# Norm gains moved behind the transposes, the identity built on GpSimd, and one product moved to other PSUM banks in a two-layer hybrid decoder

## Chip, cores and metric

The kernel runs on one core of a Trainium2 chip. The metric is device microseconds (us) of one execution. The core's engines are named as the profile names them: PE (TensorE), with PEld for its weight loads, DVE (VectorE), ACT (ScalarE), POOL (GpSimd) and SP (SyncE, here the queue that issues nearly all DMAs). Each engine takes its own instructions strictly in order.

## What is computed

Two layers of a decoder on x (256 x 1024, fp32), with a fixed memory mem (256 x 1024). Cut to what matters here:

```python
for l in range(2):
    h = rmsnorm(x, norm_g[l])
    z = h @ w_in[l]                       # 1024 -> 7968, split into many parts
    mem_kv = rmsnorm(mem, mem_norm_g[l]) @ w_mem_kv[l]   # 1024 -> 1024: keys, values
    o_a = nsa(z parts); o_b = fox(z parts); o_m = cross_attention(z part, mem_kv)
    u = sum of gate_i * (o_i @ w_branch_i[l])
    x = x + u @ w_out[l]

def rmsnorm(x, g): return x * rsqrt(mean(x * x) + 1e-6) * g
```

`norm_g` and `mem_norm_g` are the gains: one number for each of the 1024 columns and each layer.

## The kernel before

All products are fp32 in three passes. Each operand is split into a high part (fp32r) and the rest, and PE adds high x high, low x high and high x low (`gemm_steps`, lines 224, 225, 226). ACT makes the high part of a weight (line 160) and DVE the low part (line 161), two weight chunks ahead of their use. A weight chunk is 256 rows x 512 columns, 512 KB, in one of four `wraw` buffers that SP fills (line 140). A product of 1024 rows (`gemm`) is four such steps, each of 12 PE instructions, for two row tiles t of 128 tokens. Its sums lie in banks of the pool `pmm`, of which there are three. `pS` is another pool, of two banks, for scores; `pT` has two for transposes.

The activation has to stand transposed, columns on partitions. `to_T` does four PE transposes (line 329) of one row tile into one bank. Then ACT writes the high part (line 315) and DVE the low part (line 317), 512 elements wide.

The gain is a factor per column, so before the transpose it is a factor along the free axis. `gain_rows` therefore loads it broadcast to all 128 partitions, 256 KB per half. DVE multiplies mem by it in `mem_norm` (line 359) and x by it and by the row's rstd in `norm_x` (line 566). The row factor rstd of mem is applied to the results of the product. `mem_norm` also takes the sums of squares on ACT (line 372).

The order of the program: mem is loaded, normalised and transposed; `mem_kv` makes the memory's keys K and then its values V, both 1024 x 512. Beside them `norm_x` squares x on ACT (line 560), POOL makes rstd (lines 295, 296), DVE scales x and PE transposes it to hT. Then the parts of `ORDER` follow: K2 (416 columns), K1 (384), Q, and so on. After K of the memory, `on_k` squares the four heads on ACT (line 307), POOL makes their factor (lines 295, 296, 298), and DVE multiplies the bank out (line 394), which frees it. V needs two banks while K holds two of the three. So the first row tile of V can run at once and the second waits for line 394. POOL also builds the rope tables Ct and St (lines 548 to 550) in that time.

In K2 and K1, `rope_k` multiplies with the tables on DVE (lines 336 to 338) and adds the two parts on POOL (line 339). One tick later DVE multiplies by rstd (line 589), and PE transposes (line 593). The code is a list of Python calls with `later` for delayed pieces; a scheduler then sets the final order of each engine's instructions from dependencies and its own estimates.

Of the kernel before, what the change touches and what calls it, by code (L numbers as in the profile page):

```python
# [58 lines left out]
def hybrid_kernel(ctx: ExitStack, tc, I, cst_d, out_d):  # L59
# [181 lines left out]
    def gain_rows(ap, offset):  # L241

        h = [S([128, 512], tag, bufs=2) for tag in ("PTh", "PTl")]
        for i in range(2):
            nc.sync.dma_start(h[i], bcast(ap, 128, offset + i * 512, 512))
        return h

    gb0 = [S([128, 512], tag, bufs=2) for tag in ("PTh", "PTl")]
    for i, c in enumerate((0, 512)):
        nc.sync.dma_start(mrow0[:, 0, c:c + 512], I["mem"][0, 0:128, c:c + 512])  # L250
        nc.sync.dma_start(gb0[i], bcast(I["mem_norm_g"], 128, c, 512))
        if c == 0:
            nc.scalar.dma_start(cst[:, 0:128], cst_d[:, 0:128])
    nc.sync.dma_start(mrow0[:, 1], I["mem"][0, 128:256, :])
    load_w()
    load_w()
# [88 lines left out]
    def mem_load():  # L345
        mrow = S([128, NT, D], "big")
        gb = gain_rows(I["mem_norm_g"], D)
        nc.sync.dma_start(mrow, I["mem"][0].rearrange("(t p) d -> p t d", p=128))
        return mrow, gb

    def mem_norm(mrow, gb, spread):

        mT = act_pair(8, "aT")
        rm = []
        for t in range(NT):
            xn = S([128, D], "t4", bufs=2)
            for k0 in (0, 4):
                ks = slice(k0 * 128, k0 * 128 + 512)
                nc.vector.tensor_tensor(xn[:, ks], mrow[:, t, ks], gb[k0 // 4], op=ALU.mult)

                def f(xn=xn, t=t, k0=k0):
                    to_T(mT, xn[:, k0 * 128:k0 * 128 + 512], t, k0)
                if spread:
                    later(1 + 2 * t + k0 // 4, f)
                else:
                    f()
        def stats():
            for t in range(NT):
                ss = S([128, 1], "ssx", bufs=4)
                for j in range(2):  # L370
                    s2 = S([128, 1], "ssx2", bufs=4)
                    nc.scalar.activation(SQ()[:, :512], mrow[:, t, j * 512:(j + 1) * 512], AF.Square, accum_out=s2)
                    if j == 0:
                        s1 = s2
                nc.gpsimd.tensor_tensor(ss, s1, s2, op=ALU.add)
                rm.append(rstd_of(ss, D, "rm"))
            mark("mem")
        if spread:
            later(5, stats)
        else:  # L380
            stats()
        return mT, rm
# [788 lines left out]
```

## Time and profile before

| what | us |
|---|---|
| median of 3 runs (lowest, highest) | 654.85 (653.78, 655.8) |
| the profiled execution | 653.95 |
| its span in the trace | 652.2 |
| PE busy (share of the span) | 630.8 (97%) |
| DVE / ACT / POOL busy | 485.8 / 388.4 / 187.7 |

The span is from the first to the last instruction of the trace; the time of the same execution is 1.75 us longer. PE is the engine to watch: where it has no gap, no other engine's work is seen in the time. A product counts as busy until its modelled end, so the time from one start to the next is the better price of one product in a dense stretch.

### The profile page before, as it was taken

To read this page: it belongs to the slowest core of one execution; us is meant where nothing else is said; L and a number is where in the kernel's file an instruction comes from. 1 tells how busy PE (TensorE), PEld (TensorE's weight loads), DVE (VectorE), ACT (ScalarE), POOL (GpSimd) and SP (SyncE) were. 2 spreads that over 40 slices of the span, in tenths; PEclk is the share of its full clock that TensorE was granted. 3 is DMA by queue.
4 is the path that set the end of the run, shared out by engine and by line. 5 is a ranking of instruction groups with operands and counts; after the bars stand their busy time and mean duration, and the time that the engine had idled before them with its cause. 6 is when DMAs were issued, how large, how long until landed. Compare 5 with 4: busy or idle time off the path is not lost.

```text
span 652.2 us, 10316 instructions
## 1 busy us (share of the span) xinstructions
PE 630.8 (97%) x3590; PEld 539.8 (83%) x3590; DVE 485.8 (74%) x834; ACT 388.4 (60%) x817; POOL 187.7 (29%) x254
## 2 busy tenths in 40 slices
PE   5899999999998999999999999999999899999997
PEld 3688998878997888888888889987889788888886
DVE  5667889857887976856776689895598777777563
ACT  5656568654666766644566665865457475655441
POOL 2804522343222330703022234330043041133030
PEclk9999999999999999999999999999999999999999
DMA  8856556865442555465646475476644245545542
GB/s 301 216 159 182 190 162 193 201 191 171 130 120 60 154 154 161 135 222 191 215 144 182 148 224 159 135 221 172 189 141 118 65 135 158 161 130 162 162 144 83
DMA packets 74324, 106.64 MB, mean 164 GB/s; under 512 B 16032, under 2 KB 28704, under 8 KB 74272
## 3 DMA queue, kind: packets, MB, share of 16 engines
q1 hardware_dynamic: 74128, 105.92, 54.7%
q8 instruction: 28, 0.46, 0.3%
q14 instruction: 24, 0.20, 0.1%
q10 hardware_dynamic: 144, 0.07, 0.0%
HBM read 104.92 MB, written 1.05 MB: 162 GB/s over the span
## 4 chain that ended last, share of the span: by engine, by line
PE 94%; DVE 2%; POOL 2%; ACT 1%; DMA 1%; issue 0%; SPq 0%; DVEq 0%; POOLq 0%
PE mm L224 21%; PE mm L225 21%; PE mm L226 21%; PE mm L743 4%; PE O L423 4%; PE mm L746 4%; PE mm L745 3%; PE T L472 3%; PE T L329 1%; PE S L224 1%; PE S L225 1%; PE S L226 1%; PE S L916 1%; PE S L1084 1%; DMA PTl<-in_mem_norm_g_dram 1%; PE S L918 1%
## 5 line engine op out<-in xcount | busy, mean ns | idle before, releaser
L161 DVE TENSOR_TENSOR wlo<-wraw,whi 128x1024 fp32r<-128x1024 f32 (+2 forms) x184 | 232.2, 1267 | 94.2 <-ACT whi L160 89.9
L160 ACT ACTIVATE whi<-wraw 128x1024 fp32r<-128x1024 f32 (+2 forms) x184 | 191.2, 1044 | 129.5 <-PE mm L225 81.2
L224 PE MATMUL mm<-whi,aTh 128*128 128x512 f32 (+2 forms) x512 | 203.9, 398 | 5.8 <-DVE sg L728 2.9
L225 PE MATMUL mm<-whi,aTl 128*128 128x512 f32 (+2 forms) x512 | 200.5, 392 | 0.0
L226 PE MATMUL mm<-wlo,aTh 128*128 128x512 f32 (+2 forms) x512 | 194.6, 394 | 0.5 <-DVE wlo L161 0.5
L466 POOL TENSOR_TENSOR P<-P,d 128x512 f32<-128x512 f32 (+1 forms) x64 | 63.8, 1014 | 185.7 <-DVE d L458 83.1
L224 PEld LDWEIGHTS mm<-whi,aTh 128*128 128x128 f32 x512 | 97.3, 190 | 23.9 <-DVE sg L728 3.7
L226 PEld LDWEIGHTS mm<-wlo,aTh 128*128 128x128 f32 x512 | 96.8, 189 | 19.1 <-DVE wlo L161 1.3
L225 PEld LDWEIGHTS mm<-whi,aTl 128*128 128x128 f32 x512 | 97.1, 190 | 17.3
L743 PE MATMUL mm<-aTh,whi 128*128 128x256 f32 x192 | 54.5, 286 | 0.0
L745 PE MATMUL mm<-aTl,whi 128*128 128x256 f32 x192 | 54.3, 285 | 0.0
L455 ACT ACTIVATE P<-S,m 128x256 f32<-128x256 f32 (+1 forms) x112 | 47.0, 431 | 11.4 <-DVE m L452 8.2
L746 PE MATMUL mm<-aTh,wlo 128*128 128x256 f32 x192 | 52.8, 282 | 0.0
L994 POOL TENSOR_TENSOR big<-big,t 128x512 f32<-128x512 f32 x16 | 27.3, 1719 | 74.2 <-DVE t L993 74.1
L315 ACT ACTIVATE PTh<-T 128x512 fp32r<-128x512 f32 (+1 forms) x48 | 27.0, 563 | 23.8 <-PE T L472 23.5
L224 PE MATMUL mm<-whi,oTh 128*128 128x512 f32 x96 | 38.3, 404 | 0.0
L226 PE MATMUL mm<-wlo,oTh 128*128 128x512 f32 x96 | 38.2, 403 | 0.0
L225 PE MATMUL mm<-whi,oTl 128*128 128x512 f32 x96 | 38.0, 396 | 0.0
L743 PEld LDWEIGHTS mm<-aTh,whi 128*128 128x128 f32 x192 | 36.2, 188 | 0.4
L745 PEld LDWEIGHTS mm<-aTl,whi 128*128 128x128 f32 x192 | 36.2, 189 | 0.2
L746 PEld LDWEIGHTS mm<-aTh,wlo 128*128 128x128 f32 x192 | 35.7, 189 | 0.1
L452 DVE TENSOR_REDUCE m<-S 128x2 f32<-128x512 f32 (+3 forms) x64 | 31.8, 512 | 2.6 <-PE S L1084 2.4
(237 smaller groups left out, 986.1 us busy)
## 6 DMA issues: line engine op xcount, KB each, us to landing
wraw<-in_w_in_dram SPq DMA_DIRECT2D x112, 512.0 KB, 3.7
wraw<-in_w_mem_kv_dram SPq DMA_DIRECT2D x16, 512.0 KB, 5.2
wraw<-in_w_out_dram SPq DMA_DIRECT2D x16, 512.0 KB, 3.9
wraw<-in_w_branch_a_dram SPq DMA_DIRECT2D x16, 256.0 KB, 4.2
wraw<-in_w_branch_b_dram SPq DMA_DIRECT2D x8, 512.0 KB, 3.6
wraw<-in_w_branch_m_dram SPq DMA_DIRECT2D x8, 512.0 KB, 3.6
wraw<-in_w_in_dram SPq DMA_DIRECT2D x8, 408.0 KB, 3.7
wraw<-in_w_in_dram SPq DMA_DIRECT2D x8, 384.0 KB, 3.3
```

The source lines that it names most:

```text
L160: nc.scalar.activation(wh[:, :, :n], v[:, :, :n], AF.Copy)
L161: nc.vector.tensor_tensor(wl[:, :, :n], v[:, :, :n], wh[:, :, :n].bitcast(F32), op=ALU.subtract)
L224: nc.tensor.matmul(o_, hi[:, kg, ts], wh[:, k, :n], start=(kg == 0), stop=False)
L225: nc.tensor.matmul(o_, lo[:, kg, ts], wh[:, k, :n], start=False, stop=False)
L226: nc.tensor.matmul(o_, hi[:, kg, ts], wl[:, k, :n], start=False, stop=last and k == 1)
L452: nc.vector.tensor_reduce(m[:, n:n + c], heads(sp[:, o_:o_ + w * c], c), axis=AXX, op=ALU.max, negate=True)
L455: nc.scalar.activation(self.P[:, k], sp[:, k], AF.Exp, bias=m[:, n:n + 1], accum_out=d[:, n:n + 1])
L466: nc.gpsimd.tensor_tensor(P3, P3, b3(d[:, n:n + c], c, w), op=ALU.mult)
L743: nc.tensor.matmul(o_, ch, hi[:, kg, :], start=(kg == 0 and j % 2 == 0), stop=False, skip_group_check=True)
L745: nc.tensor.matmul(o_, ch, lo[:, kg, :], start=False, stop=False, skip_group_check=True)
L746: nc.tensor.matmul(o_, cl, hi[:, kg, :], start=False, stop=(kg == 7), skip_group_check=True)
L994: nc.gpsimd.tensor_tensor(uv, uv, tn, op=ALU.add)
```

## The change

It has five parts.

1. The gains of both norms and layers are loaded as 32 rows of 128 by two small DMAs on ACT's queue and turned once by PE into `gk`, 128 partitions x 32. `to_T_scaled` replaces `to_T` for mem and x: four transposes (two column blocks of both row tiles) go to one bank; then, for each block of 256 elements, ACT and DVE apply the gain as a scale per partition while they write high and low. The multiplications of line 359 and the broadcast loads go; x is scaled by rstd alone.
2. The identity is no longer loaded. POOL fills it with ones and `affine_select` keeps the diagonal.
3. mem comes in four column groups of 256 KB, alternating with the first three weight chunks; the first chunk comes and is split in two halves. Of the four transpose groups the first stands ahead of the memory's K product, and the other three are called within it. Eight products of zeros (`WARM`) stand ahead of everything on PE.
4. The squares of mem are taken once and kept for layer 1. They stand behind the four groups' code.
5. K1's sums lie in the two `pS` banks, and the add of `rope_k` moves from POOL to DVE.

```diff
+WARM = 8
@@ load_w
+        if not loaded:
+            for j in range(2):
+                nc.sync.dma_start(v[:, j], spec[0][j * 128:(j + 1) * 128])
+            spec = []
+            n = 512
@@ split_w
-        nc.scalar.activation(wh[:, :, :n], v[:, :, :n], AF.Copy)
-        nc.vector.tensor_tensor(wl[:, :, :n], v[:, :, :n], wh[:, :, :n].bitcast(F32), op=ALU.subtract)
+        for j in (slice(0, 1), slice(1, 2)) if not parts else (slice(0, k),):
+            nc.scalar.activation(wh[:, j, :n], v[:, j, :n], AF.Copy)
+            nc.vector.tensor_tensor(wl[:, j, :n], v[:, j, :n], wh[:, j, :n].bitcast(F32), op=ALU.subtract)
@@ gemm_steps
+            if t == 0 and within:
+                within.pop(0)()
@@ start of the program (was: mem and gains in halves, the identity by DMA, two weight chunks)
+    grow = S([32, 128], "tm", bufs=2)
+    for i, nm in enumerate(("mem_norm_g", "norm_g")):
+        nc.scalar.dma_start(grow[i * 16:(i + 1) * 16, :], I[nm].rearrange("l (k p) -> (l k) p", p=128))
+    nc.gpsimd.memset(cst[:, 0:128], 1.0)
+    nc.gpsimd.affine_select(out=cst[:, 0:128], in_=cst[:, 0:128], pattern=[[-1, 128]], compare_op=ALU.is_equal,
+                            fill=0.0, base=0, channel_multiplier=1)
+    for g in range(4):
+        mem_cols(mrow0, g)
+        if g < 3:
+            load_w()
+    zero = S([128, 512], "P", bufs=2, dt=F32R)
+    nc.vector.memset(zero.bitcast(F32), 0.0)
+    zp = pS()
+    for _ in range(WARM):
+        nc.tensor.matmul(zp, zero[:, 0:128], zero, start=True, stop=True)
...
+    gk = S([128, 32], "gk")
+    gp = pT()
+    nc.tensor.transpose(gp[:, 0:32], grow, ident[0:32, 0:32])
+    nc.vector.tensor_copy(gk, gp[:, 0:32])
+    def to_T_scaled(dst, src, g, gain):
+        hi, lo = dst[:2]
+        q = pT()
+        for k in range(2):
+            for t in range(NT):
+                nc.tensor.transpose(q[:, (k * 2 + t) * 128:(k * 2 + t + 1) * 128],
+                                    src(t)[:, (g * 2 + k) * 128:(g * 2 + k + 1) * 128], ident)
+        for k in range(2):
+            kg, s = g * 2 + k, q[:, k * 256:(k + 1) * 256]
+            gc = gain[:, kg:kg + 1]
+            nc.scalar.activation(hi[:, kg, :], s, AF.Copy, scale=gc)
+            nc.vector.scalar_tensor_tensor(lo[:, kg, :], s, gc, hi[:, kg, :].bitcast(F32), op0=ALU.mult, op1=ALU.subtract)
@@ rope: its add is (eng or nc.gpsimd); rope_k passes nc.vector
@@ mem_norm (layer 0: group 0 at once, 1 to 3 in `within`; layer 1: later(1 + g))
+        for g in range(4):
+            def f(g=g):
+                to_T_scaled(mT, lambda t: mrow[:, t, :], g, gk[:, l * 8:l * 8 + 8])
+    def mem_stats(mrow):
+        res = []
+        for t in range(NT):
+            ss = S([128, 1], "ssx", bufs=4)
+            nc.scalar.activation(S([128, D], "t4", bufs=2), mrow[:, t, :], AF.Square, accum_out=ss)
+            res.append(rstd_of(ss, D, "rm"))
+        return res
@@ norm_x
+            xn = [S([128, D], "t4", bufs=2) for t in range(NT)]
             for t in range(NT):
-                        nc.vector.scalar_tensor_tensor(xn[:, ks], x[t][:, ks], r, gb[k0 // 4],
-                                                       op0=ALU.mult, op1=ALU.mult)
+                later(1 + t, lambda t=t, r=r: nc.vector.tensor_scalar(xn[t], x[t], r, None, op0=ALU.mult))
+            for g in range(4):
+                later(3 + g, lambda g=g: to_T_scaled(hT, lambda t: xn[t], g, gk[:, 16 + l * 8:24 + l * 8]))
@@ run_k1
-            gemm(hT, 8, on_k1)
+            gemm(hT, 8, on_k1, bank=pS)
```

The scheduler's order moves with it, at three places. On POOL at the program's start (`cst` holds the identity in its first 128 columns, `ISA` is an instruction that the build puts ahead of the first POOL operation other than a memset), before:

```order
L272 MEMSET mhalf_75 128x16
L488 MEMSET kcT_79 128x64
L493 MEMSET KL_81 64x512 x2
L508 MEMSET gcol_153 128x4
L540 MEMSET fg_157 128x1
L780 MEMSET sTv_1579 128x128
L863 MEMSET ce_1651 128x128
L375 ISA
L375 TENSOR_TENSOR ssx_120<-ssx2_121,ssx2_124 128x1
```

and changed:

```order
L263 MEMSET cst_61 128x128
L291 MEMSET mhalf_90 128x16
L518 MEMSET kcT_98 128x64
L523 MEMSET KL_100 64x512 x2
L264 ISA
L264 AFFINE_SELECT cst_61<-cst_61 128x128
```

The `ISA`, which stood ahead of the first sum of squares, now stands ahead of the selection that makes the identity.

On ACT before, from the last transposed groups of mem to K's squares (`T_105`, `T_113` are mem's groups, `whi_205` is weight chunk 4):

```order
L160 ACTIVATE whi_169<-wraw_71 128x1024
L315 ACTIVATE aTh_84<-T_105 128x4x128
L160 ACTIVATE whi_173<-wraw_73 128x1024
L315 ACTIVATE aTh_84<-T_113 128x4x128
L160 ACTIVATE whi_177<-wraw_142 128x1024
L160 ACTIVATE whi_205<-wraw_144 128x1024
L560 ACTIVATE t4_193,ssx_194<-x0_77 128x1024
L560 ACTIVATE t4_199,ssx_200<-x1_78 128x1024
L160 ACTIVATE whi_225<-wraw_223 128x1024
```

and changed (`T_105`, `T_165`, `T_204` are the transposed groups 0, 1, 2 of mem; `big_62` is mem; chunk 4, `whi_194`, comes next):

```order
L168 ACTIVATE whi_145<-wraw_69 128x512 x2
L368 ACTIVATE aTh_103<-T_105,gk_94 128x256
L168 ACTIVATE whi_151<-wraw_73 128x1024
L368 ACTIVATE aTh_103<-T_165,gk_94 128x256
L368 ACTIVATE aTh_103<-T_105,gk_94 128x256
L168 ACTIVATE whi_155<-wraw_76 128x1024
L368 ACTIVATE aTh_103<-T_165,gk_94 128x256
L410 ACTIVATE t4_115,ssx_114<-big_62 128x1024
L410 ACTIVATE t4_121,ssx_120<-big_62 128x1024
L588 ACTIVATE t4_180,ssx_182<-x0_92 128x1024
L368 ACTIVATE aTh_103<-T_204,gk_94 128x256
L588 ACTIVATE t4_181,ssx_187<-x1_93 128x1024
```

The squares of mem, which ACT did first, now stand behind the first two groups of mem, with the squares of x close behind them and half of mem's evacuation still to come. On DVE in the same place, before:

```order
L317 TENSOR_TENSOR aTl_85<-T_105,aTh_84 128x4x128
L161 TENSOR_TENSOR wlo_174<-wraw_73,whi_173 128x1024
L317 TENSOR_TENSOR aTl_85<-T_113,aTh_84 128x4x128
L161 TENSOR_TENSOR wlo_178<-wraw_142,whi_177 128x1024
L161 TENSOR_TENSOR wlo_206<-wraw_144,whi_205 128x1024
L566 SCALAR_TENSOR_TENSOR t4_193<-x0_77,rx_196,PTh_149 128x512
L566 SCALAR_TENSOR_TENSOR t4_193<-x0_77,rx_196,PTl_150 128x512
L566 SCALAR_TENSOR_TENSOR t4_199<-x1_78,rx_202,PTh_149 128x512
L566 SCALAR_TENSOR_TENSOR t4_199<-x1_78,rx_202,PTl_150 128x512
L161 TENSOR_TENSOR wlo_226<-wraw_223,whi_225 128x1024
```

and changed:


```order
L169 TENSOR_TENSOR wlo_156<-wraw_76,whi_155 128x1024
L369 SCALAR_TENSOR_TENSOR aTl_104<-T_165,gk_94,aTh_103 128x256
L369 SCALAR_TENSOR_TENSOR aTl_104<-T_204,gk_94,aTh_103 128x256
L590 TENSOR_SCALAR t4_180<-x0_92,rx_184 128x1024
L590 TENSOR_SCALAR t4_181<-x1_93,rx_189 128x1024
L169 TENSOR_TENSOR wlo_195<-wraw_192,whi_194 128x1024
L369 SCALAR_TENSOR_TENSOR aTl_104<-T_204,gk_94,aTh_103 128x256
```

DVE had chunk 4's low part (`wlo_206`) and all low parts of mem ahead of the scaling of x. Now chunk 4 (`wlo_195`) and the low part of mem's column block 5 (the last row) stand behind both scalings of x.

On PE at the end of K1's first row tile before (`mm_580` and `mm_581` are K1's two row tiles, `T_627` and `T_667` transposes of K2's keys):

```order
L225 MATMUL mm_580<-whi_584,aTl_162 128x384
L226 MATMUL mm_580<-wlo_585,aTh_161 128x384
L593 MATMUL T_627<-cst_61,t2_541 128x128
L593 MATMUL T_667<-cst_61,t2_566 128x128
L224 MATMUL mm_581<-whi_506,aTh_161 128x384
L225 MATMUL mm_581<-whi_506,aTl_162 128x384
L226 MATMUL mm_581<-wlo_507,aTh_161 128x384
L224 MATMUL mm_581<-whi_506,aTh_161 128x384
```

and changed (`S_593` and `S_594` are K1's two row tiles, `T_640` is the first of the same transposes):

```order
L235 MATMUL S_594<-wlo_598,aTh_137 128x384
L233 MATMUL S_594<-whi_597,aTh_137 128x384
L234 MATMUL S_594<-whi_597,aTl_138 128x384
L235 MATMUL S_594<-wlo_598,aTh_137 128x384
L616 MATMUL T_640<-cst_61,t2_554 128x128
L233 MATMUL S_593<-whi_624,aTh_137 128x384
L234 MATMUL S_593<-whi_624,aTl_138 128x384
L233 MATMUL S_594<-whi_624,aTh_137 128x384
```

Both row tiles of K1 now run together. The first of the two transposes stands behind three quarters of K1, the second behind the first two products of Q.

## Rows read from the trace of the kernel before

**Rows 1.** Page, part 1: busy us (share of the span) and instructions of PE.

```profile
PE 630.8 (97%) x3590; PEld 539.8 (83%) x3590; DVE 485.8 (74%) x834; ACT 388.4 (60%) x817; POOL 187.7 (29%) x254
```

**Rows 2.** Windows: stretch, us, busy us (instructions) by engine, PEclk, DMA.

```profile
0.00:12.07 12.07, 4.15 (x16) 2.87 (x17) 4.00 (x7) 6.14 (x13) 3.92 (x18) 1.00 0.79 267
...
14.25:24.05 9.80, 9.80 (x44) 7.88 (x42) 6.95 (x9) 5.22 (x10) 5.17 (x12) 1.00 0.83 233
26.60:31.75 5.15, 2.48 (x12) 1.47 (x11) 3.19 (x5) 4.60 (x13) 4.69 (x13) 1.00 0.94 296
50.00:60.00 10.00, 8.47 (x48) 8.04 (x47) 6.97 (x29) 7.78 (x28) 3.48 (x6) 1.00 0.49 150
190.00:210.00 20.00, 18.02 (x107) 15.26 (x106) 14.73 (x31) 11.44 (x22) 4.50 (x9) 1.00 0.28 68
368.00:380.00 12.00, 10.49 (x56) 9.53 (x55) 10.05 (x36) 8.88 (x32) 4.91 (x8) 1.00 0.51 149
...
640.00:652.20 12.20, 8.39 (x37) 6.46 (x35) 3.90 (x5) 0.88 (x1) 0.00 (x0) 1.00 0.23 86
```

**Rows 3.** Waits of PE: line <- releaser: us in total, times, longest.

```profile
PE T L593 <- DVE t L589: 2.3, 2, 1.2
```

**Rows 4.** Timeline of PE, first products: start us, us, line, op, tiles.

```profile
12.07 0.80 PE L224 MATMUL mm<-whi,aTh 128*128 128x512 f32 x1
```

**Rows 5.** Timeline of PE, 24 to 25 us.

```profile
24.28 1.03 PE L329 MATMUL T<-cst,t 128*128 128x128 f32 x8
```

**Rows 6.** Timeline of PE, the start of K2.

```profile
41.54 0.36 PE L224 MATMUL mm<-whi,aTh 128*128 128x416 f32 x1
```

**Rows 7.** Timeline of ACT, the first memory quarter landed.

```profile
4.04 0.63 ACT L372 ACTIVATE sq<-big 128x512 f32<-128x512 f32 x1 [1.60 <-DMA big<-in_mem_dram]
```

**Rows 8.** Timeline of POOL, the program's start.

```profile
2.23 0.20 POOL L863 MEMSET ce<- 128x128 f32 x1
7.46 0.19 POOL L375 TENSOR_TENSOR ssx<-ssx,ssx 128x1 f32<-128x1 f32 x1 [5.04 <-ACT sq L372]
...
8.01 1.00 POOL L296 TENSOR_TENSOR rm<-rm,mhalf 128x1 f32<-128x1 f32 x1
```

**Rows 9.** Groups by form, ACT, 0 to 60 us: busy us, mean ns.

```profile
L160 ACT ACTIVATE whi<-wraw 128x1024 fp32r<-128x1024 f32 x10 | 10.4, 1054 | 7.7 <-DMA wraw<-in_w_mem_kv_dram 4.3 <-PE mm L225 3.4
L315 ACT ACTIVATE aTh<-T 128x512 fp32r<-128x512 f32 x8 | 4.6, 584 | 0.5 <-PE T L329 0.5
```

**Rows 10.** Groups by form, DVE, 0 to 60 us.

```profile
L161 DVE TENSOR_TENSOR wlo<-wraw,whi 128x1024 fp32r<-128x1024 f32 x9 | 11.0, 1224 | 5.2 <-ACT whi L160 5.2
L317 DVE TENSOR_TENSOR aTl<-T,aTh 128x512 fp32r<-128x512 f32 x8 | 5.4, 683 | 0.0
...
L566 DVE SCALAR_TENSOR_TENSOR t<-x,rx,PTh 128x512 f32<-128x512 f32 x2 | 1.6, 776 | 1.2 <-POOL rx L296 1.2
```

**Rows 11.** DMA issues, 0 to 40 us: count, KB each, median us to landing.

```profile
x<-in_x_dram SPq DMA_DIRECT2D x2, 512.0 KB, 10.3
```

**Rows 12.** Timeline of ACT, end of the squares of x.

```profile
19.27 0.19 ACT L560 ACTIVATION_READ_ACCUMULATOR t<-x 128x1 f32 x1
```

**Rows 13.** Timeline of DVE, the scaling of x behind them.

```profile
21.21 0.80 DVE L566 SCALAR_TENSOR_TENSOR t<-x,rx,PTh 128x512 f32<-128x512 f32 x1 [0.44 <-POOL rx L296]
```

**Rows 14.** Timeline of POOL, key statistics of the memory product.

```profile
28.90 0.19 POOL L295 TENSOR_SCALAR rmk<-ss 128x4 f32<-128x4 f32 x1
...
30.66 0.31 POOL L298 TENSOR_SCALAR rmk<-rmk,rm 128x4 f32<-128x4 f32 x1
```

**Rows 15.** Timeline of PE, value product of row tile 1.

```profile
31.75 0.51 PE L224 MATMUL mm<-whi,aTh 128*128 128x512 f32 x1 [1.48 <-DVE t L394]
```

**Rows 16.** Timeline of PE, the key transpose and K1's second row tile.

```profile
55.24 0.30 PE L593 MATMUL T<-cst,t 128*128 128x128 f32 x1 [1.16 <-DVE t L589]
55.91 0.42 PE L224 MATMUL mm<-whi,aTh 128*128 128x384 f32 x1 [0.36 <-DVE fz L622]
```

**Rows 17.** Windows as in group 2: behind the wait in layer 1.

```profile
519.10:522.60 3.50, 3.47 (x9) 2.71 (x10) 2.23 (x6) 2.34 (x7) 0.00 (x0) 0.53 0.00 0
```

More of the change, by code (lines that the diff above doesn't have):

```diff
@@ L178, in hybrid_kernel @@
     conts, units, pipe = [], [], [None, None]
+    within = []
     done_ = set()
@@ L228, in gemm_steps, with gemm @@
                 consume(t, o_)
+            if t == 0 and within:
+                within.pop(0)()
         tick()
-    def gemm(act, kk, consume, between=None):
-        pp = [pmm(), pmm()]
+    def gemm(act, kk, consume, between=None, bank=None):
+        bank = bank or pmm
+        pp = [bank(), bank()]
         for g in range(kk // 2):
@@ L240, in hybrid_kernel, with mem_cols @@
     mrow0 = S([128, NT, D], "big")
[L241 to L256, printed above, removed]
+    def mem_cols(mrow, g):
+        cs = slice(g * 256, (g + 1) * 256)
+        nc.sync.dma_start(mrow[:, :, cs], I["mem"][0].rearrange("(t p) d -> p t d", p=128)[:, :, cs])
+    grow = S([32, 128], "tm", bufs=2)
[13 more added lines that the diff above has]
+        nc.tensor.matmul(zp, zero[:, 0:128], zero, start=True, stop=True)
     off = [0]
@@ L338, in rope @@
         nc.vector.tensor_tensor(tmp[:, :, 32:64], src[:, :, 0:32], St[:, :, 32:64], op=ALU.mult)
-        nc.gpsimd.tensor_tensor(dst, dst, tmp, op=ALU.add)
+        (eng or nc.gpsimd).tensor_tensor(dst, dst, tmp, op=ALU.add)
     def tb(ap, nh):
@@ L346, in mem_load, with mem_norm @@
         mrow = S([128, NT, D], "big")
[L347 to L351, printed above, removed]
+        for g in range(4):
+            mem_cols(mrow, g)
+        return mrow
+    def mem_norm(l, mrow):
         mT = act_pair(8, "aT")
-        rm = []
-        for t in range(NT):
[L356 to L382, printed above, removed]
+        for g in range(4):
+            def f(g=g):
+                to_T_scaled(mT, lambda t: mrow[:, t, :], g, gk[:, l * 8:l * 8 + 8])
+                if g == (3 if l else 0):
+                    mark("mem")
+            if l:
+                later(1 + g, f)
+            elif g:
+                within.append(f)
+            else:
+                f()
+        return mT
+    def mem_stats(mrow):
+        res = []
+        for t in range(NT):
+            ss = S([128, 1], "ssx", bufs=4)
+            nc.scalar.activation(S([128, D], "t4", bufs=2), mrow[:, t, :], AF.Square, accum_out=ss)
+            res.append(rstd_of(ss, D, "rm"))
+        return res
     def mem_kv(l, mT, rm):
@@ L493, in hybrid_kernel @@
         nc.gpsimd.memset(KL[(1 - g) * 64:(2 - g) * 64, g].bitcast(F32), 0.0)
-    mT, rm = mem_norm(mrow0, gb0, False)
-    load_w()
-    load_w()
+    mT = mem_norm(0, mrow0)
+    rm = mem_stats(mrow0)
     for t in range(NT):
@@ L556, in norm_x @@
         def norm_x():
+            xn = [S([128, D], "t4", bufs=2) for t in range(NT)]
             for t in range(NT):
[L558 removed]
                 ss = S([128, 1], "ssx", bufs=4)
[L560 removed]
+                nc.scalar.activation(xn[t], x[t], AF.Square, accum_out=ss)
                 r = rstd_of(ss, D, "rx")
[L563 to L570 removed]
+                later(1 + t, lambda t=t, r=r: nc.vector.tensor_scalar(xn[t], x[t], r, None, op0=ALU.mult))
+            for g in range(4):
+                later(3 + g, lambda g=g: to_T_scaled(hT, lambda t: xn[t], g, gk[:, 16 + l * 8:24 + l * 8]))
+            later(6, lambda: mark(("h", l)))
         later(1, norm_x)
@@ L585, in rope_k @@
             kr = heads(T2()[:, :128], 2)
-            rope(kr, heads(p, 2), 2, tb(Ct[:, t, i, :], 2), tb(St[:, t, i, :], 2))
+            rope(kr, heads(p, 2), 2, tb(Ct[:, t, i, :], 2), tb(St[:, t, i, :], 2), nc.vector)
             def s1():
@@ L1138, in hybrid_kernel @@
             if l == 0 and (n, g) == (1, 1):
-                mrow, gbm = mem_load()
+                mrow = mem_load()
                 box = []
-                later(1, lambda: box.append(mem_norm(mrow, gbm, True)))
+                later(1, lambda: box.append(mem_norm(1, mrow)))
         if l == 0:
-            mT, rm = box[0]
+            mT = box[0]
     while conts or units or pipe[0] or pipe[1]:
```

11 lines of the change are left out of this document (1 added, 10 removed).

## Prediction, made before the changed kernel ran

> **What bounds the kernel now.** I read the page's busy shares first. PE is busy for 630.8 of 652.2 us [rows 1], so all that can be won without removing products is its 21.4 us of gaps. The windows show where they lie [rows 2]: 7.92 us before the first product at 12.07 (PE works 4.15 of them, on transposes), 2.67 us from 26.60 to 31.75, 1.53 us from 50 to 60 and 1.51 us from 368 to 380, 1.98 us from 190 to 210, and 3.81 us at the end. A gap of the kind of 190 to 210 returns in layer 1 at 510 to 523. The view of PE's waits then gives the causes. The gaps near 55 and 375 are the transpose of line 593, which waits twice for DVE's line 589, 2.3 us in all [rows 3]; behind it K1's second row tile waits for a bank that K2 still holds, 0.36 us [rows 16]. At 31.75 the second row tile of V waits for line 394, which frees its bank [rows 15].
>
> The change touches the first gap, the one at 27 to 32, and the two near 55 and 375. I leave the ends of the layers and the gap at 190 to 210 as they are: the orders of PE and DVE around it are the same in both programs.
>
> **The start, step by step.** What is removed here is the path from the broadcast gains over DVE's multiplications to the transposes. The first quarter of mem had landed when ACT started at 4.04 [rows 7]. The changed kernel's first memory group has the same size and the same place in the queue, so I take 4 us for it, too.
>
> The new condition is the identity. POOL's memsets ahead of the `ISA` end at about 2.3 us: in the row they end at 2.43, and the changed order has one 128x128 memset more and four fewer in front. What the `ISA` takes is in no row. POOL's next operation came 5.04 us after the memsets and was released by ACT, so the `ISA` lies between nothing and 5.04 [rows 8]. I take the long end, as nothing in the row shows it shorter: 7.3. The selection itself lies between a memset of 128x128, 0.20, and the first power, 1.00 [rows 8]; I take 0.4, near the memset, whose size it has. The identity is there at 7.75.
>
> The Trainium skill's page GPSIMD Engine Reference, section Instruction dispatch, says that the first call to freshly loaded POOL code costs about 6 us more and shows no instruction of its own. The trace's 5.04 is below that; by the page's figure all that follows would be 0.9 us later, and the estimate 650.3.
>
> Then the turn of the gains and its copy (0.4, an estimate), four transposes (0.5, half of eight in 1.03 [rows 5]) and one evacuation. A 512-wide one takes 0.58 [rows 9], so I put a 256-wide one at 0.4. The first product starts at 9.1, against 12.07 [rows 4].
>
> That gain of 3 us is not kept, because ACT becomes the queue that counts. In the changed order, from the first evacuation to the square of x's second row tile, ACT has five evacuations (2.0), two weight splits (2.1, 1.05 each [rows 9]) and four squares. A square has the width of a split; with its read of the sum (0.19 [rows 12]) I count 1.14, so 4.6. That makes 8.7 us from 8.65, and the last square ends at 17.3. From the end of the same square (19.27 + 0.19 [rows 12]) to DVE's scaling (21.21 [rows 13]) POOL took 1.75 us, so DVE starts at 19.05. The scaling of 1024 elements lies between one and two passes of line 566 (0.78 each [rows 10]); I take 1.2. Then come chunk 4's low part, 1.22 [rows 10], and a 256-wide low part, which I put at 0.45 from 0.68 for 512 [rows 10]. This is mem's block 5, and it is ready at 21.9.
>
> PE needs that block after 34 products and two groups of transposes. One product takes 0.23 us from start to start (44 products touch 9.80 us [rows 2]), so PE would be there at 9.1 + 7.8 + 1.0 = 17.9. **A new wait of about 4 us** appears inside the first product. It also covers what the clock costs: if the first ten products run at the lower level of 1.2 GHz, where nine took 3.47 us [rows 17], that is some 2 us. The eight products of zeros fit into PE's empty first 6 us and cost nothing.
>
> From 21.9 to the end of K's first row tile PE has 18 products and a group of transposes: 26.6. ACT's four squares of the keys take 1.5 us (four instructions of about 0.37). POOL's factor takes 2.1 us [rows 14], 0.3 of it for work that now stands ahead, so 1.8. Line 394 and the handover take 0.8 (30.97 to 31.75 [rows 14, 15]). The bank is free at 30.7, where it was at 31.75. PE's own path reaches the same place at 30.3, so both agree. Behind it stand 30 products and two transpose groups, 7.9 us, until K2 starts: 38.6. Two groups of transposes that were ahead of K2 before are still to come, 1.0. That makes 39.6, against 41.54 [rows 6]. **The start gives 1.9 us.**
>
> Its ends: were the `ISA` free, ACT could start 2.6 us sooner, and the start would give 4.5. With the selection at 1.00 it gives 1.3.
>
> **K2 to K1.** With K1 in the score banks its second row tile waits for nothing, and the transposes stand 6 us behind K2. The add of 0.45 to 1.15 us on POOL becomes four adds of some 0.29 on DVE per layer, which stand behind chunk 3's low part and ahead of chunk 4's. No unit uses the score banks until Q is done. Both gaps go: 1.53 + 1.51 = **3.0 us** [rows 2]. What hides DVE's extra 1.2 us is PE's work on K1, 48 products; if that cover is gone, it is paid once per layer.
>
> **At nothing.** The multiplications of mem and x in layer 1, the broadcast loads and the second squares of mem lay beside PE's full stretches. The added halves of the evacuations, 16 per layer, lengthen ACT by some 0.2 each there, and ACT is busy 60% [rows 1]. In layer 1 hT needs both row tiles, but 22 us of K and V stand in front of its use.
>
> **Sum.** 1.9 + 3.0 = 4.9 us. The profiled execution took 653.95, 1.75 more than its span; the median is 654.85. I set the sum against the middle of the two, 654.4: 649.5, and 0.1 less for rounding up the gaps: **649.4 us**.
>
> **Rivals.** (A) GpSimd is later than its row allows, for instance because its code comes while all DMA queues are full: half as long again, 7.5 us, is 2.5 later. The start gives nothing or loses 0.6: 652. For it: the row's 5.04 was bounded by ACT and not by POOL; against it: POOL then began at once. The page named above speaks for this side.
>
> (B) The K1 gap moves instead of going. DVE is then the pace-maker between K2 and Q: with four adds and all of K1's rope behind Q's low parts, PE waits for a low part of Q for as long as it waited for the transpose. Only the start is left: 652.5. For it: DVE's own share is 70% in 50 to 60 and 84% in 368 to 380 [rows 2]. Against it: the changed order has the low parts of K1's last chunk and Q's first ahead of K1's rope.
>
> (C) The identity is early (the `ISA` takes next to nothing). The start gives 4.5: 646.8. If besides the low clock behind layer 1's wait stays away, it is 645.2: PE there ran 3.50 us at a granted 0.53, which is about the lower level of 1.2 GHz, after the wait that ended at 519.1, and lost 3.50 x 0.47 = 1.6 us [rows 17]. Layer 0's gap of the same kind kept 1.00 [rows 2]. So a run may have this loss once, twice or not at all. The new wait of 4 us may bring one more, 651.
>
> (D) **Slower.** ACT is in order, and the square of x stands ahead of the evacuation of mem's third group. If x lands late, ACT stands still, and with it PE. A tile of x landed 10.3 us after its issue at about 6 to 7 us [rows 11], so near 17, and 1 MB of mem, 1.5 MB of weights and no broadcast gains now stand ahead of it: some 14 us. Each us past 16.2 is paid in full. It turns slower by over 0.3% (2 us, about what a measurement of this kernel can tell from no change) where x's second tile lands 6.9 us later, after 23; at 25 the time is 658. Against it: less is queued ahead of x than before.
>
> **How the numbers follow.** My forecast 0.58, A 0.14, B 0.10, C 0.13, D 0.05. Of these, faster by over 0.3% (below 652.4) are 0.55 of the forecast's, 0.08 of A's, 0.06 of B's and all of C's: 0.82. Slower is D alone, 0.05; the rest, 0.13, is within 0.3%. The range leaves out the lower end of C (0.05), D and the upper parts of A and B (0.05): 645.5 to 653.3. The forecast's own range, with the `ISA` and the clock as open, is 646.8 to 651.
>
> **What would show it.** The profile after should show the identity's selection ending near 7.7, the first product near 9, a wait inside the first product for DVE's low part that ends near 22, K2's first product near 39, and no wait of a K transpose or of K1 near 55 and 375. A selection that ends before 4 is C, after 10 A; a wait in Q for a low part is B; an ACT that waits for x is D. I am wrong in kind if PE's gaps between 60 and 640 grow by more than 2 us, since the order there has changed too and I have priced none of it.

## Result and profile after

The changed kernel takes 647.99 us (median of 4 runs, 646.9 to 648.83) against 655.26 (653.78 to 655.8): ratio 0.9892, 95% interval 0.9866 to 0.9918. The forecast was 649.4. The sum is near by luck: of its two terms one was not paid at all, and what came in its place, 4.2 us from the places of tiles, stood in no term.

The page after, part 1, and windows after (columns as in [rows 2]; the third number from the end is the granted clock, 1.00 for 2.4 GHz and 0.50 for 1.2; 202.5 to 206 follows the wait near 201 us):

```profile
PE 630.4 (97%) x3599; PEld 541.5 (84%) x3599; DVE 485.5 (75%) x849; ACT 389.1 (60%) x822; POOL 173.7 (27%) x240
```

```profile
9.70:14.40 4.70, 4.70 (x12) 3.31 (x12) 2.95 (x4) 3.81 (x6) 0.00 (x0) 0.50 1.05 397
50.00:60.00 10.00, 10.00 (x57) 9.54 (x56) 8.90 (x30) 8.46 (x33) 3.49 (x7) 1.00 0.82 244
100.00:116.00 16.00, 14.62 (x118) 12.07 (x117) 14.82 (x26) 13.03 (x35) 6.48 (x6) 1.00 0.60 153
190.00:210.00 20.00, 18.02 (x98) 15.10 (x97) 14.45 (x29) 10.71 (x21) 4.45 (x9) 0.91 0.29 69
366.00:378.00 12.00, 12.00 (x65) 11.10 (x64) 10.97 (x39) 9.99 (x36) 4.67 (x8) 1.00 0.78 228
414.00:432.00 18.00, 16.65 (x134) 13.83 (x133) 16.75 (x29) 14.68 (x40) 7.57 (x6) 1.00 0.60 168
...
202.50:206.00 3.50, 3.50 (x10) 2.73 (x9) 2.29 (x6) 2.62 (x6) 0.74 (x2) 0.53 0.00 0
```

The gaps near 55 and 375 are gone: PE fills 50 to 60 and 366 to 378. But two gaps are new, 1.38 us in 100 to 116 and 1.35 us in 414 to 432. PE's waits in 100 to 116 (line <- releaser: us, times, longest) name them:

```profile
PE mm L235 <- DVE wlo L169: 0.7, 2, 0.4
PE T L502 <- DVE PTl L341: 0.5, 1, 0.5
PE T L502 <- POOL P L496: 0.2, 1, 0.2
```

The start, in the timeline of PE (first transposes, first product, three waits, K2):

```profile
5.05 0.65 PE L363 MATMUL T<-cst,big 128*128 128x128 f32 x4
9.02 1.09 PE L363 MATMUL T<-cst,big 128*128 128x128 f32 x4 [3.31 <-DMA big<-in_mem_dram]
9.76 1.20 PE L233 MATMUL mm<-whi,aTh 128*128 128x512 f32 x2
...
20.98 0.50 PE L233 MATMUL mm<-whi,aTh 128*128 128x512 f32 x1 [0.30 <-ACT whi L168]
...
29.23 0.50 PE L233 MATMUL mm<-whi,aTh 128*128 128x512 f32 x1 [0.33 <-ACT whi L168]
...
30.49 0.50 PE L235 MATMUL mm<-wlo,aTh 128*128 128x512 f32 x1 [0.52 <-DVE wlo L169]
...
39.45 0.35 PE L233 MATMUL mm<-whi,aTh 128*128 128x416 f32 x1
```

and of POOL:

```profile
1.18 1.09 POOL L523 MEMSET KL<- 64x512 f32 x2
2.32 0.29 POOL L264 TENSOR_SCALAR_AFFINE_SELECT cst<-cst 128x128 f32<-128x128 f32 x1
```

The identity was ready at 2.6 us. What PE waited for, 3.31 us, was mem's second quarter: all eight transposes of the first two groups stand ahead of the first product. K2 began at 39.45, before at 41.54 [rows 6].

These differences don't make the gain. At the wait of 1.46 us near 201 us (before, then after) the changed kernel is only 2.1 us ahead:

```profile
203.31 0.51 PE L224 MATMUL mm<-whi,aTh 128*128 128x512 f32 x1 [1.46 <-DVE sg L728]
201.22 0.50 PE L233 MATMUL mm<-whi,aTh 128*128 128x512 f32 x1 [1.46 <-DVE sg L751]
```

All of this lead was there when K2 began: from K2 to this wait both kernels took 161.77 us. What is left shows in stretches without any wait. In layer 1, twelve products before, from the first row's start to the last's:

```profile
319.71 0.39 PE L224 MATMUL mm<-whi,aTh 128*128 128x512 f32 x1
...
322.51 0.39 PE L224 MATMUL mm<-whi,aTh 128*128 128x512 f32 x1
```

and twelve after:

```profile
322.00 0.39 PE L233 MATMUL mm<-whi,aTh 128*128 128x512 f32 x1
...
324.72 0.39 PE L233 MATMUL S<-whi,aTh 128*128 128x512 f32 x1
```

2.80 / 12 = 0.233 us before, 2.72 / 12 = 0.227 after, both at a granted clock of 1.00. Over some 1,200 neighbouring pairs of such products the mean pitch (the time from one start to the next) is 233.1 ns before and 229.2 after. 3.9 ns x 1,200 makes 4.7 us, more than either term of the forecast. The modelled duration (0.39) does not show it; only starts do.

### The profile page after: what moved, and what is told of

The parts are those of the page before. It is cut to its first block, busy times and chain, and to the rows that moved or that the text cites. A ratio compares the mean times of both kernels' runs of the same rounds, so it can differ in the third digit from the quotient of the medians.

```text
span 647.1 us, 10360 instructions
## 1 busy us (share of the span) xinstructions
PE 630.4 (97%) x3599; PEld 541.5 (84%) x3599; DVE 485.5 (75%) x849; ACT 389.1 (60%) x822; POOL 173.7 (27%) x240
## 4 chain that ended last, share of the span: by engine, by line
PE 91%; DVE 3%; ACT 3%; issue 1%; DMA 1%; SPq 0%; ACTq 0%
PE mm L235 20%; PE mm L233 20%; PE mm L234 19%; PE mm L766 4%; PE mm L768 4%; PE mm L769 4%; PE O L453 3%; PE T L502 3%; PE S L235 2%; PE S L233 2%; PE S L234 2%; DMA wraw<-in_w_mem_kv_dram 1%; DVE wlo L169 1%; PE S L1107 1%; PE S L939 1%
## 5 line engine op out<-in xcount | busy, mean ns | idle before, releaser
L169 DVE TENSOR_TENSOR wlo<-wraw,whi 128x1024 fp32r<-128x1024 f32 (+3 forms) x185 | 235.9, 1278 | 100.0 <-ACT whi L168 95.8
L168 ACT ACTIVATE whi<-wraw 128x1024 fp32r<-128x1024 f32 (+3 forms) x185 | 191.9, 1040 | 128.7 <-PE mm L234 64.5
L233 PE MATMUL mm<-whi,aTh 128*128 128x512 f32 (+1 forms) x480 | 190.2, 399 | 3.6 <-DVE sg L751 2.9
L234 PE MATMUL mm<-whi,aTl 128*128 128x512 f32 (+1 forms) x480 | 189.2, 394 | 0.1
L235 PE MATMUL mm<-wlo,aTh 128*128 128x512 f32 (+1 forms) x480 | 185.0, 398 | 1.9 <-DVE wlo L169 1.9
L496 POOL TENSOR_TENSOR P<-P,d 128x512 f32<-128x512 f32 (+1 forms) x64 | 59.6, 943 | 186.6 <-DVE d L492 76.7
L233 PEld LDWEIGHTS mm<-whi,aTh 128*128 128x128 f32 x480 | 91.1, 190 | 21.1 <-DVE sg L751 3.7
L235 PEld LDWEIGHTS mm<-wlo,aTh 128*128 128x128 f32 x480 | 91.0, 190 | 20.6 <-DVE wlo L169 3.7
L234 PEld LDWEIGHTS mm<-whi,aTl 128*128 128x128 f32 x480 | 91.2, 190 | 17.6 <-DVE aTl L369 1.1
L485 ACT ACTIVATE P<-S,m 128x128 f32<-128x128 f32 (+1 forms) x112 | 47.1, 431 | 11.9 <-DVE m L482 11.8
L233 PE MATMUL mm<-whi,oTh 128*128 128x512 f32 x96 | 38.6, 405 | 0.0
```

The source lines that it names most:

```text
L168: nc.scalar.activation(wh[:, j, :n], v[:, j, :n], AF.Copy)
L169: nc.vector.tensor_tensor(wl[:, j, :n], v[:, j, :n], wh[:, j, :n].bitcast(F32), op=ALU.subtract)
L233: nc.tensor.matmul(o_, hi[:, kg, ts], wh[:, k, :n], start=(kg == 0), stop=False)
L234: nc.tensor.matmul(o_, lo[:, kg, ts], wh[:, k, :n], start=False, stop=False)
L235: nc.tensor.matmul(o_, hi[:, kg, ts], wl[:, k, :n], start=False, stop=last and k == 1)
L485: nc.scalar.activation(self.P[:, k], sp[:, k], AF.Exp, bias=m[:, n:n + 1], accum_out=d[:, n:n + 1])
```

## Experiments

Ratios are to the kernel before, timed in turns on the same chip; in brackets the 95% interval. Pitches are means of all intervals under 300 ns between neighbouring 512-wide products of one kind after 20 us.

**r1: the changed kernel again.** No edit.

> The changed kernel once more, timed in turns with the kernel before on one chip. It fixes the size of the gain and asks one thing of the trace: in the first pair of traces, dense stretches of products without any wait ran at a start-to-start of about 228 ns after and 231 ns before (the mean over 210 to 640 us differs by some 3 ns per product, 3 to 4 us in all). If that belongs to the change, it shows again here against the other kernels of this set, and the ratio is 0.987 to 0.991. If it belongs to the chip or the execution, the ratio is nearer to what the waits alone explain, 0.992 to 0.995, that is 3.5 to 5 us.

Measured: 646.92, ratio 0.9885 [0.9863, 0.9907], pitch 229.1. The pitch belongs to the kernel. The low clock after 202 us does not: r1's trace has 1.00 there.

**r2 and r3: part 5 undone, and part 5 alone.**

```diff
# r2, from the changed kernel
-            rope(kr, heads(p, 2), 2, tb(Ct[:, t, i, :], 2), tb(St[:, t, i, :], 2), nc.vector)
+            rope(kr, heads(p, 2), 2, tb(Ct[:, t, i, :], 2), tb(St[:, t, i, :], 2))
-            gemm(hT, 8, on_k1, bank=pS)
+            gemm(hT, 8, on_k1)
# r3: the same lines, and the bank argument of gemm, put into the kernel before
```

> Everything but part 5: K1's sums go back to the pool of three banks and the add of its rope back to POOL. Theory of the prediction: part 5 is worth 3.0 us, so this kernel takes 3.0 us more than the changed one (651.0 against 648.0) and PE waits again some 1.2 us for the K transposes behind K2 in both layers. Rival, from the trace of the changed kernel: part 5 also moved the compression of the keys to a later place, and PE got three new waits of 0.5 to 0.7 us each per layer behind it (104 to 115 us and 419 to 430 us), some 3.6 us in all with what follows them; then part 5 is worth nothing, this kernel stands within 0.7 us of the changed one, and those waits are absent here.

> The kernel before with part 5 alone (K1's sums in the score banks, the add of the key rope on DVE). Theory of the prediction: 3.0 us faster than before, 652.3, ratio 0.9954, with no waits at K1 and no new ones. Rival: the waits at K1 go (3.0 to 3.7 us) and the new ones of 0.5 to 0.7 us each, three per layer, come (3.6 us): ratio 0.999 to 1.001.

Measured: r2 646.97, 0.9888 [0.9867, 0.9908]; r3 656.14, 1.0025 [1.0007, 1.0042]. Without part 5 the time is that of r1, and part 5 alone costs 1.6 us. The windows of r1:

```profile
50.00:60.00 10.00, 10.00 (x57) 9.47 (x56) 9.16 (x30) 8.45 (x33) 3.76 (x7) 1.00 0.82 240
100.00:116.00 16.00, 14.59 (x121) 12.10 (x120) 14.83 (x26) 13.03 (x34) 6.48 (x6) 1.00 0.58 147
```

and of r2:

```profile
50.00:60.00 10.00, 8.62 (x47) 7.83 (x47) 7.87 (x30) 7.99 (x28) 3.25 (x6) 1.00 0.46 132
100.00:116.00 16.00, 16.00 (x128) 13.71 (x127) 14.99 (x25) 12.96 (x31) 4.16 (x3) 1.00 0.72 164
```

They mirror each other: 1.38 us of gap at 50 to 60 without part 5, 1.41 us at 100 to 116 with it. The prediction's term of 3.0 us is paid back 50 us later. The loss of r3 lies mostly ahead of K2 (42.90 there, 41.54 before): another wait of 1.9 us for a low part came up at 28.8, and the clock was at its lower level from 29.0 to 32.4 behind it.

**r4 and r8: the clock at the start.** r4 adds eight products of zeros that need mem's first quarter; r8 takes the first eight away.

```diff
# r4
+                z2 = S([128, 512], "P", bufs=2, dt=F32R)
+                nc.vector.tensor_scalar(z2[:, 0:128], mrow[:, 0, 0:128], 0.0, None, op0=ALU.mult)
+                for _ in range(8):
+                    nc.tensor.matmul(zp, z2[:, 0:128], zero, start=True, stop=True)
# r8
-WARM = 8
+WARM = 0
```

> The changed kernel with eight more products of zeros on PE behind the first eight; they need the first quarter of mem, so they fall into PE's wait of 3.3 us for the second quarter (5.7 to 9.0 us). In the changed kernel the clock is at its lower level from the end of that wait to 14.4 us, which costs PE some 2.3 us there. If PE alone sets the pace of the first product, keeping the clock up gives 2 us or more (646 or less). If ACT's queue sets it (ACT has no idle time of note from 10.3 to 20.9 us), PE only comes earlier to the wait for the weights' high part at 21 us, which grows by as much, and the time changes by less than 0.8 us. If the products of zeros do not raise the clock, it stays low to about 14 us as before and nothing changes either; the granted clock between 9 and 14 us tells these two apart.

> The changed kernel without the eight products of zeros at its start. Theory: they do nothing for the time, since the clock is at its lower level while they run, PE then waits for mem's second quarter, and the first products run at the lower level anyway until about 14 us; the time stays within 0.5 us of the changed kernel and the clock comes up at 14 us again. Rival: they bring the clock up earlier; without them it stays low for 2 us or more longer and the time grows by 1 to 2 us.

Measured: r4 651.86, 0.9961 [0.9946, 0.9977]; r8 650.22, 0.9922 [0.9906, 0.9938]. Both lose against the changed kernel, and neither by the clock at the start as expected: the scheduler gave both another order. In r4 two whole weight splits stand ahead of the first evacuation on ACT, and ACT waits there for their weights:

```profile
10.05 1.06 ACT L169 ACTIVATE whi<-wraw 128x1024 fp32r<-128x1024 f32 x1 [3.77 <-DMA wraw<-in_w_mem_kv_dram]
12.14 1.06 ACT L169 ACTIVATE whi<-wraw 128x1024 fp32r<-128x1024 f32 x1 [1.03 <-DMA wraw<-in_w_mem_kv_dram]
13.11 0.46 ACT L369 ACTIVATE aTh<-T,gk 128x256 fp32r<-128x256 f32 x1
```

PE then waited 4.96 us for the second group's transposes, and the clock was at its lower level from 11.3 to 21.5. So r4 leaves the price of the clock open.

In r8 the products reached the upper level sooner, not later: at 11.5 us, in the changed kernel at 14.6. The rows of the changed kernel's start (above) show why the zeros are no help. The four transposes right behind them took 0.65 us, the next four, behind the wait of 3.31 us, 1.09. So in this trace the zeros did bring the clock up (granted 1.00 from 4.4 to 7.8), and it fell again (0.50 from 7.8 to 14.6) while PE was waiting for mem. It differs from run to run: in r1, the same kernel, the upper level came back at 12.9, and in the six traces with these zeros and this order on PE (changed, r1, r6, r7, r10, r11) between 12.2 and 14.6. r8 is a single trace beside them. PE was 2.3 us early in r8, and gave it all back:

```profile
31.34 0.47 PE L233 MATMUL mm<-whi,aTh 128*128 128x512 f32 x1 [2.31 <-DVE t L424]
```

The cause is on POOL in r8, which is still at the rope tables' work when K's squares are done at 25.6:

```profile
26.64 1.20 POOL L569 TENSOR_TENSOR fg<-gcol 64x1 f32<-64x1 f32 x1
...
28.73 0.19 POOL L319 TENSOR_SCALAR rmk<-ss 128x4 f32<-128x4 f32 x1
```

K's factor starts at 28.73 there. In the changed kernel it starts at 28.32, where K's squares end at 28.2 and POOL came free at 28.1: both were just in time. So an earlier PE alone frees the bank no sooner. Behind the wait the clock fell (granted 0.57 from 31.4 to 35.4), another 1.7 us, and K2 began at 40.81. Whether a start with PE's old order and a higher clock would gain was not tried.

**r5 to r7, r10 to r12: places in SBUF.** Both kernels were built with unused tiles. They move the operands of PE and every tile behind them; apart from POOL's memsets of the unused tiles, all engines keep their instructions and order.

```diff
     x = [S([128, D], f"x{t}") for t in range(NT)]
+    nc.gpsimd.memset(S([128, 32], "padA"), 0.0)      # r5, r6, r12; r11 with 8 columns
         St = S([128, NT, 3, 64], "St")
+        if l == 0:
+            nc.gpsimd.memset(S([128, 32], "padB"), 0.0)  # r5, r6, r10; r11 with 56
         VN = S([128, 2, NT, 2, 128], "VN", dt=F32R)
+        if l == 0:
+            nc.gpsimd.memset(S([128, 48], "padC"), 0.0)  # r7; r9 and r12 have it too; r10 40, r11 32
```

> The kernel before with two unused tiles of 128 bytes per partition. The first lies ahead of the transposed activations aTh and aTl, the second between them and the weights whi and wlo. So aTh begins at byte 65248 of a partition, as in the changed kernel, not at 65120; modulo 256 that is 224 (where whi and wlo begin in all kernels) in place of 96. Nothing else changes but places. Theory: the place of the stationary operand sets the pitch of the products, so products of aTh and aTl go from 232 to 233 ns down to about 229 ns from start to start, oTh and oTl stay at about 233, and the kernel takes 3 to 4.5 us less, ratio 0.993 to 0.995. Rival: the pitch comes from something else that the start of the changed kernel brought (fewer DMAs, the gains, other places); then the ratio is 0.999 to 1.001.

> The changed kernel with the same two unused tiles: aTh now begins at byte 65376, 96 modulo 256 as in the kernel before, and whi and wlo stay at 224. Theory: the pitch goes back to 232 to 233 ns and the kernel takes 3 to 4.5 us more than the changed one (650 to 651.4, ratio 0.993 to 0.995). If the place at 65248 itself or an order of tiles counts and not the rest modulo 256, the pitch may take a third value. Rival: no change (0.9885).

> The changed kernel with an unused tile of 192 bytes ahead of oTh and oTl, so that these also begin at 224 modulo 256 (173792 in place of 173600). Theory: the 288 products of oTh and oTl in the branches, at 231 and 236 ns now, go to about 228 ns, which gives some 1.2 to 1.5 us (645.6, ratio 0.9865). Rival: only the place of aTh against itself or against the pool's start counts; then nothing changes within 0.3 us.

> The changed kernel with aTh and aTl left at 224 modulo 256, whi and wlo moved to 96 and oTh and oTl to 64, by two unused tiles. Theory: the place of the stationary operand alone counts, so products of aTh stay at about 229 ns; those of oTh then show what 64 gives. Rival: stationary and moving operand have to lie at the same place modulo 256; then the products of aTh rise to about 233 ns. One look, read from the pitch in the trace, not from the time.

> The changed kernel with aTh and aTl at 0 modulo 256, oTh and oTl at 160, and whi and wlo left at 224. If only 224 (equal to the weights) is good, both pitches are about 233 ns and the time is 650 to 653. If 0 is as good or better than 224, the products of aTh are at 229 ns or less, and the time is 646 to 648 or below.

> The kernel of r9 with one unused tile of 128 bytes ahead of all these operands: aTh, aTl, oTh, oTl, whi and wlo now all begin at 96 modulo 256, where aTh with weights at 224 ran at 233 ns. Theory from r5 to r11: the places of the two operands against each other count; equal places are good wherever they are, so the pitches stay at about 229 ns and the time at that of r9 (643 to 645, ratio 0.983 to 0.986). Rival: 224 itself is good for both and 96 for neither; then the pitches are 233 ns and the time is 648 to 651.

The first byte of the operands in a partition, modulo 256, and what was measured (aT: aTh and aTl, the stationary operand; w: whi and wlo, the moving one; r9 is told below):

| kernel | aT | oT | w | pitch aT, ns | pitch oT, ns | ratio [95%] |
|---|---|---|---|---|---|---|
| before | 96 | 32 | 224 | 233.1 | 233.7 | 1 |
| r5 | 224 | 32 | 224 | 229.6 | 233.7 | 0.9936 [0.9919, 0.9953] |
| r1 (changed) | 224 | 32 | 224 | 229.1 | 233.6 | 0.9885 [0.9863, 0.9907] |
| r6 | 96 | 32 | 224 | 232.8 | 233.5 | 0.9975 [0.9960, 0.9991] |
| r7 | 224 | 224 | 224 | 229.1 | 229.6 | 0.9876 [0.9856, 0.9895] |
| r10 | 224 | 64 | 96 | 232.8 | 233.6 | (a single run, 652.87) |
| r11 | 0 | 160 | 224 | 233.3 | 230.8 | 0.9953 [0.9937, 0.9970] |
| r9 | 224 | 224 | 224 | 229.4 | 228.8 | 0.9842 [0.9819, 0.9865] |
| r12 | 96 | 96 | 96 | 229.2 | 228.5 | 0.9834 [0.9810, 0.9859] |

256 unused bytes in the kernel before give 4.2 us (651.0). The same bytes in the changed kernel cost 5.9 (0.9975 less 0.9885, of 655). The pitch alone accounts for 4.2 of the first (3.5 ns x 1,209) and for 4.5 of the second (3.7 ns x 1,217); the other 1.4 it leaves open. The pitch follows the places of the two operands against each other: equal modulo 256 gives 228.5 to 229.6 in every case, at 224 and at 96; 128 bytes apart gives 232.8 to 233.1; the stationary operand 64 bytes below the other (r11's oT) gives 230.8, and 64 above (oT at 32), 32 above (r11's aT) or 32 below (r10's oT) 233.3 to 233.7. r10 moved the weights against aT and lost the gain; r12 moved all together and kept it. That 256 is the length that counts can be read from two pairs: 96 and 224 are equal modulo 128, and slow; in r5 the weights lie 2,304 bytes higher than in the changed kernel with aTh at the same byte, which is no multiple of 512, and both are fast. r7's 0.6 us against r1 lies inside the intervals, its pitch of oT does not. The rule is no further tested than this table, and the 256-wide products did not follow it (124.0 ns before, 124.7 after). One stretch of r12, twelve products in 2.72 us:

```profile
318.46 0.39 PE L235 MATMUL mm<-wlo,aTh 128*128 128x512 f32 x1
...
321.18 0.39 PE L235 MATMUL S<-wlo,aTh 128*128 128x512 f32 x1
```

and of r6, twelve in 2.80:

```profile
320.83 0.39 PE L233 MATMUL mm<-whi,aTh 128*128 128x512 f32 x1
...
323.63 0.39 PE L233 MATMUL mm<-whi,aTh 128*128 128x512 f32 x1
```

Before, `aTh` began at byte 65120. The new tile `gk` of 128 bytes stands ahead of it now, and the weights moved down by 2,048, which keeps their 224. The gain in pitch is an accident of the allocation. Why the chip is quicker at equal places, no run shows.

**r9: the banks without the add on DVE.**

```diff
# from r7
-            rope(kr, heads(p, 2), 2, tb(Ct[:, t, i, :], 2), tb(St[:, t, i, :], 2), nc.vector)
+            rope(kr, heads(p, 2), 2, tb(Ct[:, t, i, :], 2), tb(St[:, t, i, :], 2))
```

> The changed kernel with oTh and oTl placed as in r7, and of part 5 only the banks: K1's sums stay in the score banks, the add of the key rope goes back to POOL. It asks whether the new waits between 104 and 115 us (and 419 and 430 us) come with the banks or with the add on DVE, whose four adds per layer also move the compression of the keys. Theory: with the banks, because the key transposes then stand later in PE's order; the three waits stay and the time is that of r7 (ratio 0.987 to 0.988). Rival: with the add; the waits go, the gain of some 3 us that the prediction saw in part 5 appears, and the ratio is 0.983 to 0.985. Third: the add on POOL comes late beside POOL's other work, and a wait for the K transposes returns; then it is 0.988 or more.

Measured: 643.82, 0.9842 [0.9819, 0.9865]; r12, the same but for its places, 642.34, 0.9834 [0.9810, 0.9859]. Both windows of r9 are full:

```profile
50.00:60.00 10.00, 10.00 (x57) 9.50 (x56) 8.86 (x28) 8.48 (x33) 5.30 (x10) 1.00 0.79 238
100.00:116.00 16.00, 16.00 (x143) 13.69 (x142) 15.21 (x24) 13.43 (x32) 7.26 (x5) 1.00 0.75 198
```

So the banks remove the gaps at K1, and the add on DVE brings the new ones. Against r7 that is 2.2 us, with intervals that overlap a little (0.9856 to 0.9865). This version beats both kernels. DVE is no less busy in this stretch than in r1 (15.21 against 14.83), so DVE's load there is not the cause. What is left is the order that the scheduler makes around those adds; that is argued and not shown, and by which step of it was not tried.

## Why the prediction was right in the sum and wrong in its terms

The forecast was 1.9 for the start and 3.0 for K2 to K1. The runs give nothing for part 5 (r1 against r2), 4.2 for places (r5) and 3.1 for the start (r2 against r5, 0.9936 less 0.9888; uncertain by about 2). r1 measured 7.5 (0.0115 x 655). That these terms add up to 7.3 proves nothing, since the last is what r2 leaves beside r5. Counted as the prediction counts, the start gave less in the first pair of traces: K2 at 39.45, and 0.9 for the eight transposes that still stand behind it, against 41.54, so 1.2. In r5, with the orders of the kernel before, K2 came at 42.88, since the clock rose at 16.7 there and at 14.1 before; against r1's 39.18 that makes 2.8. So the start's worth lies between 1.2 and 2.8 by the traces, as the clock comes. The sum was right by luck: 3.0 that was not paid stood where 4.2 came from a cause that no step had.

- **Identity.** Taken at the long end, 7.75; it was there at 2.6. The `ISA` cost at most the 0.05 us between the memset's end (2.27) and the selection. That is rival C's condition, but not its price: the step from four transposes and one evacuation to the first product left out that the second group's transposes come first, and those waited for mem until 9.02. The first product came at 9.76, forecast 9.1. The Trainium skill's page GPSIMD Engine Reference, section Instruction dispatch, gives about 6 us for the first call to freshly loaded POOL code; this trace shows no such time ahead of the selection, and no run tells whether the selection is code of that kind.
- **The new wait inside the first product.** The end of the chain was right, the wait's size not, and the wait that showed was another. The chain came as told: x's last square with its read ended at 18.30 (forecast 17.3), the second scaling began at 19.31 (19.05), two low parts of mem ran from 21.26 to 22.13 (21.9 for block 5). PE lost 0.24 us to block 5 (two starts 0.47 apart, at 21.31 and 21.79) and not 4, since it came at 20.7 and not at 17.9. About 0.7 of this is the later start and 2.35 the clock, at 0.50 for 4.70 us. The row of 0.30 at 20.98 is a wait for ACT's high part of a weight chunk, which the prediction did not have. It said that the wait covers the clock's price; in fact the clock ate the wait.
- **To K2.** K's first squares began at 26.73 (26.6 forecast for the end of the row tile), line 424 ended at 31.43 (bank free at 30.7). POOL's factor began at 28.32 and took 2.4 us to line 424 where the sum had 1.8. Two waits for one chunk's high and low parts, 0.85 us, were not foreseen. K2 came at 39.45, forecast 38.6. That PE's own path and the bank agree was the useful sentence: r8 shows that being earlier on PE buys nothing there.
- **K2 to K1.** The failed step. That both gaps go was right, to the row. But the prediction took the adds on DVE as hidden by PE's work on K1 and looked only there; if the cover went, it said, DVE's 1.2 us would be paid once per layer. The new waits, 1.38 and 1.35 us, have that size, 50 us behind K1. The prediction named the case (PE's gaps between 60 and 640 growing, as the order there was not priced) but set the mark at 2 us net: before they were 1.98 + 1.51 + 1.98 = 5.47, after 6.69, so 1.2 net hid 2.7 of new ones. Rival B had the kind of wait, a low part from DVE, and what it costs, all of part 5's gain, but the wrong place.
- **Missing term.** No step asked where the operands lie. The trace of the kernel before has the slow pitch, but nothing in it to compare with; the traces and allocations of two builds side by side show it.
- **Clock behind the wait of each layer.** As said, it comes or not: in the kernel before it cost layer 1 [rows 17], in the changed kernel's profiled run layer 0 (0.53), in r1 neither.

Rivals A and D did not come: nothing on POOL was late, and ACT did not wait for x.

## What to carry to other kernels

When a change adds or removes tiles, compare where the operands of the dense products begin in a partition and read the start-to-start pitch of a stretch without waits in both traces, before any term is put down to the edit itself. A gap that closes is a gain only if PE is still early at the next joint: count idle time over the whole span, old gaps and new ones apart. And time a bundle's parts alone: here one half of part 5 was worth some 2 us (r9 against r7) and the other half cost as much.

## What the hardware showed that was not expected

- The pitch of 512-wide products depends on the places of stationary and moving operand against each other: about 229 ns where they are equal modulo 256 bytes, about 233 at 128 bytes apart, at the same granted clock.
- Eight products of zeros at the start raised the clock only for a moment: in the changed kernel it was granted at 1.00 from 4.4 to 7.8 us and at 0.50 from 7.8 to 14.6, after PE had waited for mem from 5.7 to 9.0. In r6, r10 and r11 the transposes right behind the zeros still ran at the lower level (0.213 us from start to start, 0.109 in the changed kernel). The first products reached the upper level at 12.2 to 14.6 us in six traces with the zeros and at 11.5 in the one without (r8).
- A low part of 128x1024 took 1.22 us with POOL idle. Beside POOL's multiplications of line 496 it took up to 1.99, in the changed kernel just ahead of the new waits:

```profile
107.13 1.75 DVE L169 TENSOR_TENSOR wlo<-wraw,whi 128x1024 fp32r<-128x1024 f32 x1 [0.54 <-ACT whi L168]
...
109.47 1.99 DVE L169 TENSOR_TENSOR wlo<-wraw,whi 128x1024 fp32r<-128x1024 f32 x1 [0.30 <-ACT whi L168]
```

```profile
106.76 1.04 POOL L496 TENSOR_TENSOR P<-P,d 128x512 f32<-128x512 f32 x1 [3.78 <-DVE d L492]
109.34 1.04 POOL L496 TENSOR_TENSOR P<-P,d 128x512 f32<-128x512 f32 x1 [1.54 <-DVE d L492]
```

The Trainium skill's page SBUF — State Buffer, section SBUF: two separate sides, says that a DVE operation with two inputs in SBUF and a GpSimd operation that reads SBUF exclude each other; these rows agree: POOL's multiplications began first and ran 0.67 and 0.91 us into the low parts, which took 0.53 and 0.77 longer. The second low part ended at 111.46, and PE's wait of 0.37 us for it at 111.51. But the slowing alone does not make a wait: in r9 two low parts beside such multiplications took 3.44 us in place of some 2.4, and PE did not wait.

```profile
105.61 3.44 DVE L169 TENSOR_TENSOR wlo<-wraw,whi 128x1024 fp32r<-128x1024 f32 x2 [0.55 <-ACT whi L168]
```
